# The expert stage's routing, gathers and one-hot places moved and reshaped in a two-block transformer kernel

## The chip, the cores and the metric

One core of a Trainium2 chip runs the whole program. The metric is the device time of one execution in microseconds; "before" is the median of three runs. The profile is of one execution of its own.

## What is computed

Two blocks follow each other on one sequence of 256 tokens of width 1024. The change touches only the second block, and in it the expert stage, which runs once in each of its two layers (l = 0, 1), between two layer norms:

```python
x = layer_norm(ALPHA * x + memory_cross_attention(x, mem, xq, xkv, xo), ln2_g, ln2_b)
x = layer_norm(ALPHA * x + grouped_moe(x, router_w, router_bias, e_gate, e_up, e_down), ln3_g, ln3_b)

def grouped_moe(x, ...):            # 16 experts in 4 groups
    scores = softmax(x @ router_w); biased = scores + router_bias
    # best group by the sum of its two best experts; in it, the two best experts
    ...
    for e in range(16):
        he = silu(x @ w_gate[e]) * (x @ w_up[e])
        y = y + combine[:, e:e+1] * (he @ w_down[e])
```

All arithmetic is float32. Each expert has three matrices of 1024 x 512 (2 MB each), so a layer's experts are 96 MB.

## The kernel before, in words

**Weights.** `Weights` (line 31) is a planner: all weights are 1 MB slabs in a fixed order, loaded on SyncE's DMA queue (`load`, line 66) into whatever slot came free first (`add`, `leave`). In an expert loop there are 14 slots in layer 0 and 16 in layer 1: 4 `raws`, 2 or 3 `EARLY`, 3 or 4 `MORE`, one in the place of `x`, 4 in the place of the `split` tiles. Expert slabs are used as they are (`whole`). All other weights are split before use into a high part (ScalarE, line 111) and a low part (VectorE, or GpSimd where `pool_every` says so, line 117); `next` splits `ahead` units in advance, `pace` sets `ahead`, `reach` and `settle` split at once.

**Fills.** In layer 0, key and value products of the next layer's cross attention (`key_steps`, `value_steps`) are run as fillers where TensorE would wait: `fill(n)` runs n of them. `norm2` has six in layer 0 and none in layer 1. They read `memt`, the memory's parts, which lie in the same four `turn` tiles as the gathered tokens; `memory_parts` (line 1616) makes them again after layer 0's experts.

**Routing (`moe`, line 2043).** After the second norm's statistics ScalarE scales the rows (`scale`), VectorE and GpSimd apply the norm's gain and bias to them in place (`gain`), and `both` splits them into `xth` and `xtl`, tokens on partitions. Beside that VectorE works through some twenty small operations that end in `sel` (line 2142), the chosen experts. Two matmuls (`rk`, line 2150) count the ranks; `code` is each token's place in its expert, at most 64 a pass, and a rank above 64 goes to an overflow path behind a branch (`tc.If`, line 2378) after the loop.

**The expert loop (line 2340).** Per group of four experts: `one_hot` (line 2179) makes the matrix `P2` on VectorE, `weights` (line 2200) sums each slot's share on TensorE, `turned` (line 2186) makes the transposed one-hots, `gather` (line 2216) brings the group's tokens into `XG`, in four banks evicted alternately by VectorE and ScalarE. Per expert: `into` (gate and up products, two abreast in halves of the array), `hidden` (transposes, silu, product), `down`, and `scatter` two experts later into four PSUM accumulators `y`. `scaled` adds ALPHA times the rows in three split passes. In layer 1 `last_gains` makes the last norm's gain and bias rows on TensorE. Small steps are put into the stream of weight units by a list of due times (`after`, `unit`, `rest`). The order of issue in the text of the program is the order on each engine: nothing is rescheduled. PSUM has four working banks (`bank`) in turn.

The rows' names: `P` is `P2`, `turn` is `XG`, `raw`, `w` and `x` are slots with slabs.

Of the kernel before, what the change touches and what calls it, by code (L numbers as in the profile page):

```python
# [30 lines left out]
class Weights:  # L31
# [27 lines left out]
    def fill(self):  # L59
        while self.loaded < len(self.dims):  # L60
            self.free = [f for f in self.free if f[1] is None or self.loaded < f[1]]
            if not self.free:
                return
            self.load(*self.free.pop(0))
# [340 lines left out]
def named(t, parts):  # L405

    out, o = {}, 0
    for name, n in parts:
# [11 lines left out]
        ("norm1", 1): 7}  # L420
# [12 lines left out]
def body(ctx, tc, nc, A, out):  # L433
# [896 lines left out]
    def pair(b):  # L1330
        return slice(2 * b, 2 * b + 2)
# [284 lines left out]
    def memory_parts():  # L1616

        memt = S2["memt"] = memory_tiles()
        for b in range(4):
            memt.cut(b, S2["memf"][:, pair(b), :], nc.gpsimd)  # L1620
# [422 lines left out]
    def moe(l, st, norm, steps):  # L2043
# [12 lines left out]
        ia = rt.tile([P, 2, P], F32R, name="ia")  # L2056
        nc.gpsimd.tensor_scalar(ia[:, 0, :], ident, ALPHA, None, op0=OP.mult)
        nc.vector.scalar_tensor_tensor(ia[:, 1, :], ident, ALPHA, ia[:, 0, :].bitcast(F32), op0=OP.mult, op1=OP.subtract)
# [4 lines left out]
        def small(n, name):  # L2063
            t = rt.tile([P, 2 * n], F32, name=name)
            return t.rearrange("p (t n) -> p t n", t=2)
# [11 lines left out]
        W.settle()  # L2077
        fill(1)
        XT = Parts(keep.tile([P, KD, T], F32R, name="xh"), keep.tile([P, KD, T], F32R, name="xl"))
# [7 lines left out]
        def gain(h, t, eng, part=slice(2)):  # L2087
            cs = slice(h * 512, (h + 1) * 512)
            for i, op in ((0, OP.mult), (1, OP.add))[part]:
                eng.tensor_tensor(whole[t][:, cs], whole[t][:, cs], norm.gb[:, i, cs], op=op)  # L2090

        def both(h, t, eng):
            cs = slice(h * 512, (h + 1) * 512)
            if (h, t) != (0, 0):
                nc.scalar.activation(xth[:, t, cs], whole[t][:, cs], AF.Copy)
            eng.tensor_tensor(xtl[:, t, cs], whole[t][:, cs], xth[:, t, cs].bitcast(F32), op=OP.subtract)
# [5 lines left out]
        gain(0, 0, V_, slice(1))  # L2102
        scale(0, 1)
        gain(0, 1, nc.gpsimd)
        scale(1, 1)
        scale(1, 0)
# [38 lines left out]
        gain(0, 0, V_, slice(1, 2))  # L2145
        both(0, 1, nc.gpsimd)
        nc.scalar.activation(xth[:, 0, 0:512], whole[0][:, 0:512], AF.Copy)
# [3 lines left out]
        nc.tensor.matmul(rk[:, 16:32], onesb, sel[:, 0, :], start=False, stop=True, skip_group_check=True)  # L2151
        code = small(16, "code")
# [5 lines left out]
        def count_late():  # L2158

            V_.tensor_scalar(late, code, 64.0, None, op0=OP.is_gt)  # L2160
            V_.tensor_reduce(nl, late.rearrange("p t n -> p (t n)"), op=OP.add, axis=AX.X)
            V_.tensor_tensor(late, late, comb, op=OP.mult)
            pb = bank()
            nc.tensor.matmul(pb[0:1, 0:1], nl, ones[:, 0:1], start=True, stop=True)
            V_.tensor_copy(flag, pb[0:1, 0:1])
# [43 lines left out]
        def gather(g, b, eng):  # L2209

            pb = bank()
            for j in range(2):
                c = 2 * b + j
                for i, a in enumerate((xth, xtl)):
                    for t in range(2):
                        nc.tensor.matmul(pb[:, j * T:(j + 1) * T], a[:, t, c * P:(c + 1) * P], P2s[g][:, t, :, 0:64],
                                         start=(j == 0 and i == 0 and t == 0), stop=(i == 1 and t == 1),
                                         skip_group_check=True)
            dst = XG[b][:, g % 2].rearrange("p c e s -> p (c e s)")
            if eng is nc.scalar:  # L2220
                nc.scalar.activation(dst, pb, AF.Copy)  # L2221
            else:
                eng.tensor_copy(dst, pb)


        due, count = [], [0]

        def after(n, *fs):
            due.extend((count[0] + n, f) for f in fs)

        def unit(name):
            now = [f for n, f in due if n <= count[0]]
            due[:] = [d for d in due if d[0] > count[0]]
            for f in now:
                f()
            count[0] += 1
            return W.whole(f"{name}{l}")

        def rest():
            while due:  # L2240
                due.sort(key=lambda d: d[0])
                due.pop(0)[1]()

        def into(e):

            pb = bank()
            for r in range(2):
                (wg, free_g), (wu, free_u) = unit("gate"), unit("up")
                for k in range(4):
                    if e == 0 and k % 2 == 0 and r + k:  # L2250
                        gather(0, 2 * r + k // 2, (V_, nc.scalar)[k // 2])
                    c = 4 * r + k
                    x_e = XG[c // 2][:, (e // 4) % 2, c % 2, e % 4, :]
                    for o, w in ((pb[0:64], wg), (pb[64:P], wu)):
                        nc.tensor.matmul(o, x_e, w[:, k, :], start=(c == 0), stop=(c == KD - 1), skip_group_check=True)  # L2255
                free_g()
                free_u()
            s = mo.tile([P, 512], F32, name="s", bufs=2)
            nc.scalar.activation(s, pb, AF.Copy)  # L2259
            return s  # L2260
# [27 lines left out]
        def scaled(i):  # L2288

            t, h = divmod(i, 2)  # L2290
            for k, a in ((0, xth), (0, xtl), (1, xth)):
                nc.tensor.matmul(y[i], ia[:, k, :], a[:, t, h * 512:(h + 1) * 512], start=False, stop=False,
                                 skip_group_check=True)

        def scatter(e):
            o = outs.pop(e)
            for t in range(2):
                for i in range(2):
                    for h in range(2):
                        hs = slice(64 * h, 64 * h + 64)  # L2300
                        nc.tensor.matmul(y[2 * t + h], PTs[e][hs, t * P:(t + 1) * P], o[hs, i, :],
                                         start=(e == 0 and i == 0), stop=False, skip_group_check=True)

        def last_gains(i):

            pb = bank()
            at = col[f"l{l}_ln3_{'gb'[i // 2]}_2"][0] + 4 * (i % 2)
            for c in range(4):
                nc.tensor.matmul(pb[:, c * P:(c + 1) * P], vcol[:, at + c:at + c + 1].to_broadcast([P, P]), ident,
                                 start=(c == 0), stop=(c == 3), skip_group_check=True)  # L2310
            nc.scalar.activation(norm.gb[:, i // 2, 512 * (i % 2):512 * (i % 2) + 512], pb, AF.Copy)
# [3 lines left out]
        one_hot(1, 0, 64)  # L2315
        nc.scalar.activation(codeb, code, AF.Copy)
        both(0, 0, V_)
        gain(1, 0, V_)
        gain(1, 1, nc.gpsimd)
        fill(8)  # L2320
        W.add(SlotOfSplit(), 4, W.end(f"down{l}") - 6)
        gather(0, 0, V_)
        both(1, 0, V_)
        both(1, 1, nc.gpsimd)
# [10 lines left out]

        after(1, lambda: one_hot(0, 64, 64), lambda: one_hot(1, 64, 64))
        after(2, shares)
        after(3, weights)
        after(8, count_late)
        for e in range(17):  # L2340

            g, j = divmod(e, 4)
            if e < 16:
                s = into(e)
            else:
                rest()
            if e > 1:
                scatter(e - 2)
            if e < 16 and j < 2:
                turned(j)  # L2350
            if e < 12:
                if j == 1:
                    one_hot, weights, soon = places(g + 1)
                    one_hot(0)
                    one_hot(1)
                    weights()
                if j > 1:
                    for b in (2 * j - 4, 2 * j - 3):
                        gather(g + 1, b, (V_, nc.scalar)[b % 2])
                if j == 3:  # L2360
                    turned = soon
            if e in (4, 6, 8, 10):
                scaled(e // 2 - 2)
                if last:
                    last_gains(e // 2 - 2)
            if e > 0:
                down(e - 1)
            if e < 16:
                hidden(e, s)
        rest()  # L2370
# [7 lines left out]
        with tc.If(over > 0):  # L2378
            with tc.tile_pool(name=f"ov{l}", bufs=1) as ov:

                for b in range(4):
# [8 lines left out]
                    V_.tensor_copy(x[:, pair(b), :], two(pb))  # L2390
# [42 lines left out]
    def second(xs):  # L2433
# [11 lines left out]
        with ExitStack() as st:  # L2445
            steps = chained(key_steps(), value_steps())
            y = moe(0, st, norm, steps)
# [3 lines left out]
        memory_parts()  # L2451
# [122 lines left out]
```

## Time and profile before

| | us |
|---|---|
| runs shown | 2162.61, 2173.63, 2176.61 |
| median | 2173.63 |
| profiled execution | 2169.32 |
| its span, first to last instruction | 2167.1 |

The two expert loops lie at about 1464 to 1706 and 1906 to 2151 us of the span. PE is TensorE's matmuls, PEld its weight loads, DVE VectorE, ACT ScalarE, POOL GpSimd, SP SyncE. PEclk is the granted clock as a share of 2.4 GHz. A wait names the engine and line that waits, then what ended it.

### The profile page before, as it was taken

The numbers are of one execution on the slowest core, as the hardware profiler recorded it, in microseconds if no ns is written. First come the engines' busy times: TensorE is split into PE (matmuls) and PEld (weight loads), VectorE is DVE, ScalarE is ACT, GpSimd is POOL, SyncE is SP. The second block draws the span as 40 slices with busy tenths as digits, with TensorE's granted clock in tenths as the row PEclk, the third lists the DMA queues.
The fourth block names the chain that finished last, engine by engine and source line by source line (L and its number), as shares of the span: only waits on it lengthen the run. The fifth ranks groups of instructions, "written<-read, shape, count | busy, mean of one in ns | idle before, by whom it ended". The sixth has DMA issues, their size and how long they took to land. (4 is left out here: it accounts for less than half of the span.)

```text
span 2167.1 us, 39266 instructions
## 1 busy us (share of the span) xinstructions
PE 2036.2 (94%) x16734; PEld 1696.3 (78%) x16734; DVE 1063.7 (49%) x1648; ACT 795.2 (37%) x1294; POOL 309.4 (14%) x392
## 2 busy tenths in 40 slices
PE   8999999999999999999999989998999899879996
PEld 8999888899999998888999979983434598733442
DVE  5556765655565557655655576562111276431112
ACT  5444432544454444424444544431111344211111
POOL 2112121111121112211111222110000402010000
PEclk9999999999999999999999999999999999989998
DMA  6454321254545543212544424559999445489993
GB/s 256 176 187 174 136 78 43 88 186 175 186 168 193 193 177 132 74 60 79 221 183 176 172 102 159 179 202 377 418 419 416 180 156 195 168 335 418 406 401 117
DMA packets 63209, 441.93 MB, mean 204 GB/s; under 512 B 6960, under 2 KB 7728, under 8 KB 10416
## 3 DMA queue, kind: packets, MB, share of 16 engines
q1 hardware_dynamic: 60704, 433.30, 52.3%
q10 hardware_dynamic: 1744, 3.90, 0.5%
q8 instruction: 136, 2.23, 0.4%
q0 software_dynamic: 576, 2.10, 0.3%
q14 instruction: 49, 0.40, 0.1%
HBM read 438.22 MB, written 1.05 MB: 203 GB/s over the span
## 5 line engine op out<-in xcount | busy, mean ns | idle before, releaser
L117 DVE TENSOR_TENSOR w<-raw,w 128x1024 fp32r<-128x1024 f32 (+1 forms) x426 | 520.3, 1246 | 227.5 <-ACT w L111 227.2
L530 PE MATMUL pb<-xh,w 128*128 128x256 f32 x2032 | 587.7, 289 | 3.6 <-ACT w L111 2.8
L531 PE MATMUL pb<-xl,w 128*128 128x256 f32 x2032 | 581.2, 286 | 7.9 <-DVE xl L1408 4.6
L532 PE MATMUL pb<-xh,w 128*128 128x256 f32 x2032 | 580.7, 286 | 7.6 <-DVE w L117 7.4
L111 ACT ACTIVATE w<-raw 128x1024 fp32r<-128x1024 f32 (+1 forms) x438 | 444.0, 1046 | 198.2 <-PE pb L532 108.9
L531 PEld LDWEIGHTS pb<-xl,w 128*128 128x128 f32 x2032 | 394.4, 194 | 11.6 <-DVE xl L1408 5.1
L532 PEld LDWEIGHTS pb<-xh,w 128*128 128x128 f32 x2032 | 394.2, 194 | 10.9 <-DVE w L117 10.8
L530 PEld LDWEIGHTS pb<-xh,w 128*128 128x128 f32 x2032 | 394.2, 194 | 10.1 <-ACT w L111 3.5
L532 PE MATMUL ab<-hh,w 128*128 128x256 f32 x704 | 197.9, 281 | 0.0
L530 PE MATMUL ab<-hh,w 128*128 128x256 f32 x704 | 197.9, 281 | 0.0
L531 PE MATMUL ab<-hl,w 128*128 128x256 f32 x704 | 196.3, 279 | 0.0
L2255 PE MATMUL pb<-raw,turn 128*64 128x512 f32 x712 | 178.6, 605 | 5.9 <-ACT turn L2221 2.7
L663 POOL TENSOR_TENSOR h<-sg,gu 128x256 f32<-128x256 f32 x88 | 80.8, 919 | 607.6 <-ACT sg L661 607.6
L2255 PEld LDWEIGHTS pb<-raw,turn 128*64 128x64 f32 x712 | 53.6, 138 | 106.6 <-issue 98.4
L530 PEld LDWEIGHTS ab<-hh,w 128*128 128x128 f32 x704 | 132.5, 188 | 0.2 <-issue 0.2
L531 PEld LDWEIGHTS ab<-hl,w 128*128 128x128 f32 x704 | 132.5, 188 | 0.0
L532 PEld LDWEIGHTS ab<-hh,w 128*128 128x128 f32 x704 | 132.2, 188 | 0.0
L659 DVE TENSOR_TENSOR gu<-pb,rr 128x512 f32<-128x512 f32 x88 | 60.7, 691 | 124.8 <-PE pb L532 119.8
L661 ACT ACTIVATE sg<-gu 128x256 f32<-128x256 f32 x88 | 36.7, 418 | 207.8 <-DVE gu L659 207.7
L2259 ACT ACTIVATE s<-pb 128x512 f32<-128x512 f32 x32 | 19.1, 598 | 204.5 <-PE pb L2255 204.5
L2281 PE MATMUL pb<-raw,h 128*64 128x512 f32 x368 | 94.0, 656 | 0.0
L2191 DVE TENSOR_SCALAR PT<-pb,C 128x512 fp32r<-128x512 f32 x16 | 12.0, 751 | 112.8 <-PE pb L2186 112.8
(563 smaller groups left out, 3155.4 us busy)
## 6 DMA issues: line engine op xcount, KB each, us to landing
raw<-in_wpack_dram SPq DMA_DIRECT2D x353, 1024.0 KB, 6.1
w<-in_wpack_dram SPq DMA_DIRECT2D x44, 1024.0 KB, 9.4
x<-in_wpack_dram SPq DMA_DIRECT2D x13, 1024.0 KB, 10.0
gb<-in_vecs_dram POOLq DMA_DIRECT2D x4, 512.0 KB, 5.5
C<-in_c_dram SPq DMA_DIRECT2D x1, 1041.0 KB, 16.2
xin<-in_x_dram SPq DMA_DIRECT2D x2, 512.0 KB, 5.7
mem<-in_mem_dram ACTq DMA_DIRECT2D x1, 1024.0 KB, 9.3
out_dram<-xout SPq DMA_DIRECT2D x4, 256.0 KB, 2.1
```

Source lines behind the costliest of these rows:

```text
L111: self.nc.scalar.activation(h, src, AF.Copy)
L117: (self.nc.gpsimd if pool else self.nc.vector).tensor_tensor(lo, src, h.bitcast(F32), op=OP.subtract)
L530: nc.tensor.matmul(o, wh, xh, start=first, stop=False, skip_group_check=True)
L531: nc.tensor.matmul(o, wh, xl, start=False, stop=False, skip_group_check=True)
L532: nc.tensor.matmul(o, wl, xh, start=False, stop=last, skip_group_check=True)
L659: nc.vector.tensor_tensor(gu, two(pb), rr[:, None, :].to_broadcast([P, 2, T]), op=OP.mult)
L661: nc.scalar.activation(sg, gu[:, 0, :], AF.Silu)
L663: nc.gpsimd.tensor_tensor(h, sg, gu[:, 1, :], op=OP.mult)
L2191: V_.tensor_scalar(PT, two(pb), c2["slotp"], None, op0=OP.is_equal)
L2255: nc.tensor.matmul(o, x_e, w[:, k, :], start=(c == 0), stop=(c == KD - 1), skip_group_check=True)
L2259: nc.scalar.activation(s, pb, AF.Copy)
L2281: nc.tensor.matmul(pb[64 * n:64 * n + 64], h[:, 2 * r + k, :], w[:, k, n * 512:(n + 1) * 512], start=(r == 0 and k == 0), stop=(r == 1 and ...
```

## The change

Gain and bias of norm 2 no longer go into the rows before the split: `xth` and `xtl` are parts of the plain normalized rows, and gain and bias (now per partition) are applied where `gather` evicts a bank, half by VectorE, half by ScalarE. The rows with gain, which `scaled` needs, are made later by eight VectorE steps in expert 0; `scaled` is then one full float32 product per bank, all four in expert 1. GpSimd has no work in the routing. In layer 1 thirty warm-up matmuls stand ahead of `rk`. Two gathers instead of one stand ahead of the loop. In a group, one-hots are made in its first expert, weights in its second, and the gathers are spread 0, 1, 2, 1 over the four. `scatter` follows `down` instead of preceding it. The count of late tokens moves behind expert 2. `memory_parts` is called in expert 15 of layer 0 with VectorE instead of GpSimd, and two fill units are split ahead of the branch. `last_gains` becomes a broadcast load from HBM on GpSimd's queue, at expert 13. The list of due times is gone. In the overflow path the evictions apply gain and bias too.

```diff
-        ("norm1", 1): 7}
+        ("norm1", 1): 7, ("route", 1): 30}
-            memt.cut(b, S2["memf"][:, pair(b), :], nc.gpsimd)
+            memt.cut(b, S2["memf"][:, pair(b), :], nc.vector)
...
-        ia = rt.tile([P, 2, P], F32R, name="ia")
...
+        ia = rt.tile([P, P], F32, name="ia")
+        nc.gpsimd.tensor_scalar(ia, ident, ALPHA, None, op0=OP.mult)
...
         W.settle()
+        W.pace(0)
         fill(1)
...
+        def first_part(h, t):
+            cs = slice(h * 512, (h + 1) * 512)
+            nc.scalar.activation(xth[:, t, cs], whole[t][:, cs], AF.Copy)
+        def second_part(h, t):
+            cs = slice(h * 512, (h + 1) * 512)
+            V_.tensor_tensor(xtl[:, t, cs], whole[t][:, cs], xth[:, t, cs].bitcast(F32), op=OP.subtract)
...
-        gain(0, 0, V_, slice(1))
         scale(0, 1)
-        gain(0, 1, nc.gpsimd)
-        scale(1, 1)
-        scale(1, 0)
+        first_part(0, 0)
+        first_part(0, 1)
+        for t in range(2):
+            scale(1, t)
+        for t in range(2):
+            first_part(1, t)
...
         fill(2)
-        gain(0, 0, V_, slice(1, 2))
-        both(0, 1, nc.gpsimd)
-        nc.scalar.activation(xth[:, 0, 0:512], whole[0][:, 0:512], AF.Copy)
+        warm("route", l)
...
+        second_part(0, 0)
         code = small(16, "code")
...
-            dst = XG[b][:, g % 2].rearrange("p c e s -> p (c e s)")
...
+            for j in range(2):
+                dst = XG[b][:, g % 2, j].rearrange("p e s -> p (e s)")
+                gv, bv = vec(norm.g, 0, 2 * b + j), vec(norm.b, 0, 2 * b + j)
+                if j:
+                    nc.scalar.activation(dst, pb[:, T:], AF.Identity, scale=gv, bias=bv)
+                else:
+                    V_.tensor_scalar(dst, pb[:, :T], gv, bv, op0=OP.mult, op1=OP.add)
...
-                    if e == 0 and k % 2 == 0 and r + k:
-                        gather(0, 2 * r + k // 2, (V_, nc.scalar)[k // 2])
+                    if e == 0 and c in (2, 4):
+                        gather(0, c // 2 + 1)
...
-            for k, a in ((0, xth), (0, xtl), (1, xth)):
-                nc.tensor.matmul(y[i], ia[:, k, :], a[:, t, h * 512:(h + 1) * 512], start=False, stop=False,
+            nc.tensor.matmul(y[i], ia, whole[t][:, h * 512:(h + 1) * 512], start=True, stop=False, skip_group_check=True)
...
+                nc.gpsimd.dma_start(norm.gb[:, i, :], rows[at:at + D].partition_broadcast(P))
...
+        second_part(0, 1)
         nc.scalar.activation(codeb, code, AF.Copy)
-        both(0, 0, V_)
-        gain(1, 0, V_)
-        gain(1, 1, nc.gpsimd)
+        W.pace(2)
         fill(8)
...
-        gather(0, 0, V_)
-        both(1, 0, V_)
-        both(1, 1, nc.gpsimd)
+        gather(0, 0)
+        second_part(1, 0)
+        gather(0, 1)
+        second_part(1, 1)
...
         for e in range(17):
...
+            if e == 0:
+                one_hot(0, 64, 64)
+                one_hot(1, 64, 64)
+                shares()
+                weights()
+                late_shares()
+                for i in range(4):
+                    gain(i % 2, i // 2)
+            if e == 1:
+                for i in range(4):
+                    scaled(i)
+            if e == 15 and ending is not None:
+                ending()
+            if e == 16:
+                scatter(14)
+            if e > 0:
+                down(e - 1)
+            if e == 16:
+                W.pace(2)
+                W.reach(2)
+                W.settle()
+            elif e > 1:
                 scatter(e - 2)
             if e < 16 and j < 2:
                 turned(j)
+            if e == 2:
+                count_late()
             if e < 12:
-                if j == 1:
+                if j == 0:
                     one_hot, weights, soon = places(g + 1)
                     one_hot(0)
                     one_hot(1)
+                elif j == 1:
                     weights()
-                if j > 1:
-                    for b in (2 * j - 4, 2 * j - 3):
-                        gather(g + 1, b, (V_, nc.scalar)[b % 2])
+                for b in ([], [0], [1, 2], [3])[j]:
+                    gather(g + 1, b)
...
-            if e in (4, 6, 8, 10):
-                scaled(e // 2 - 2)
-                if last:
-                    last_gains(e // 2 - 2)
-            if e > 0:
-                down(e - 1)
+            if last and e == 13:
+                last_gains()
             if e < 16:
                 hidden(e, s)
```

## Rows read from the trace of the kernel before

**Rows 1.** the page, parts 1 and 5: engines, and splitting a weight

```profile
PE 2036.2 (94%) x16734; PEld 1696.3 (78%) x16734; DVE 1063.7 (49%) x1648; ACT 795.2 (37%) x1294; POOL 309.4 (14%) x392
...
L117 DVE TENSOR_TENSOR w<-raw,w 128x1024 fp32r<-128x1024 f32 (+1 forms) x426 | 520.3, 1246 | 227.5 <-ACT w L111 227.2
...
L111 ACT ACTIVATE w<-raw 128x1024 fp32r<-128x1024 f32 (+1 forms) x438 | 444.0, 1046 | 198.2 <-PE pb L532 108.9
```

**Rows 2.** stretches: us; busy PE, PEld, DVE, ACT, POOL; PEclk, DMA, GB/s

```profile
1520.00:1540.00 20.00, 20.00 (x109) 8.73 (x107) 2.52 (x4) 2.76 (x5) 0.00 (x0) 1.00 1.00 413
...
1540.00:1560.00 20.00, 18.20 (x88) 7.43 (x88) 4.27 (x8) 2.52 (x5) 0.00 (x0) 0.91 1.01 423
...
1464.40:1480.30 15.90, 13.73 (x66) 6.53 (x67) 4.33 (x12) 1.19 (x2) 1.04 (x1) 0.89 0.89 371
...
1890.00:1900.00 10.00, 0.20 (x2) 0.10 (x1) 8.95 (x29) 3.91 (x7) 6.03 (x6) 0.66 1.02 427
...
1905.90:1922.30 16.40, 14.19 (x66) 6.59 (x67) 4.41 (x12) 1.27 (x3) 1.57 (x1) 0.86 0.57 220
```

**Rows 3.** waits of PE, layer 0, 1430:1720: us, times, longest

```profile
PE pb L2200 <- DVE P L2179: 5.4, 6, 1.5
...
PE pb L2150 <- DVE sel L2142: 3.6, 1, 3.6
...
PE pb L2255 <- ACT turn L2221: 1.4, 2, 0.7
...
PE pb L2255 <- ACT xh L2095: 0.8, 1, 0.8
...
PE pb L2255 <- DVE turn L2223: 0.8, 1, 0.8
...
PE pb L2164 <- DVE nl L2161: 0.7, 1, 0.7
```

**Rows 4.** waits of PE, layer 1, 1880:2167

```profile
PE pb L2150 <- DVE sel L2142: 11.3, 1, 11.3
...
PE pb L2255 <- DVE turn L2223: 1.6, 2, 0.8
```

**Rows 5.** timeline at experts 5 and 15, layer 0: start, us, engine

```profile
1550.08 1.28 DVE L2179 TENSOR_TENSOR P<-C,code 128x512 fp32r<-128x512 f32 x2
...
1550.91 0.24 PE L2200 MATMUL pb<-comb,P 128*128 128x2 f32 x1 [1.54 <-DVE P L2179]
...
1552.55 5.04 PE L2281 MATMUL pb<-raw,h 128*64 128x512 f32 x16
...
1693.57 3.65 PE L2281 MATMUL pb<-raw,h 128*64 128x512 f32 x16
```

**Rows 6.** timeline of both layers' routing

```profile
1445.82 0.18 DVE L2124 TENSOR_TENSOR two_max<-bi 128x16 f32<-128x16 f32 x1
...
1893.87 1.22 DVE L2124 TENSOR_TENSOR two_max<-bi 128x16 f32<-128x16 f32 x1
...
1895.14 1.28 POOL L2090 TENSOR_TENSOR ol<-ol,gb 128x512 f32<-128x512 f32 x1
...
1899.94 1.12 DVE L2138 TENSOR_SCALAR top<-ahead 128x32 f32<-128x32 f32 x1
```

**Rows 7.** timeline: expert 4 of layer 1, and warm-ups after the middle norm

```profile
1977.52 0.48 PE L2292 MATMUL ab<-xh,ia 128*128 128x512 f32 x1
...
1978.30 1.06 PE L2309 MATMUL pb<-ident,vcol 128*128 128x128 f32 x8
...
1727.98 1.24 PE L523 MATMUL pb<-identb 128*128 128x512 bf16 x5 [1.03 <-ACT x L1452]
```

**Rows 8.** groups by line from 1300 on: a gain step on DVE

```profile
L2090 DVE TENSOR_TENSOR oh<-oh,gb 128x512 f32<-128x512 f32 x8 | 5.5, 687 | 1.8 <-ACT oh L2085 1.8
```

**Rows 9.** stretches: the middles of both loops, columns as in rows 2

```profile
1528.00:1682.00 154.00, 150.39 (x760) 60.54 (x758) 21.55 (x38) 18.58 (x35) 0.00 (x0) 0.98 1.00 413
...
1943.00:2117.00 174.00, 170.39 (x884) 72.79 (x882) 23.24 (x40) 23.73 (x44) 0.00 (x0) 0.98 0.99 403
```

More of the change, by code (lines that the diff above doesn't have):

```diff
@@ L2041, in tile, with moe @@
             return split.tile([P, 2, 1024], F32, name="w").rearrange("p c t -> p (c t)")
-    def moe(l, st, norm, steps):
+    def moe(l, st, norm, steps, ending=None):
         nonlocal x
@@ L2054, in moe @@
         fill = filler(steps, l, "norm2")
-        ia = rt.tile([P, 2, P], F32R, name="ia")
-        nc.gpsimd.tensor_scalar(ia[:, 0, :], ident, ALPHA, None, op0=OP.mult)
-        nc.vector.scalar_tensor_tensor(ia[:, 1, :], ident, ALPHA, ia[:, 0, :].bitcast(F32), op0=OP.mult, op1=OP.subtract)
+        ia = rt.tile([P, P], F32, name="ia")
+        nc.gpsimd.tensor_scalar(ia, ident, ALPHA, None, op0=OP.mult)
         trib, onesb = rt.tile([P, P], BF16, name="trib"), rt.tile([P, P], BF16, name="onesb")
@@ L2085, in scale, with gain @@
             nc.scalar.activation(whole[t][:, cs], norm.zt[2 * t + h], AF.Identity, scale=r[:, t:t + 1], bias=nm[:, t:t + 1])
-        def gain(h, t, eng, part=slice(2)):
+        def first_part(h, t):
             cs = slice(h * 512, (h + 1) * 512)
-            for i, op in ((0, OP.mult), (1, OP.add))[part]:
-                eng.tensor_tensor(whole[t][:, cs], whole[t][:, cs], norm.gb[:, i, cs], op=op)
-        def both(h, t, eng):
+            nc.scalar.activation(xth[:, t, cs], whole[t][:, cs], AF.Copy)
+        def second_part(h, t):
             cs = slice(h * 512, (h + 1) * 512)
-            if (h, t) != (0, 0):
-                nc.scalar.activation(xth[:, t, cs], whole[t][:, cs], AF.Copy)
-            eng.tensor_tensor(xtl[:, t, cs], whole[t][:, cs], xth[:, t, cs].bitcast(F32), op=OP.subtract)
+            V_.tensor_tensor(xtl[:, t, cs], whole[t][:, cs], xth[:, t, cs].bitcast(F32), op=OP.subtract)
+        def gain(h, t):
+            cs = slice(h * 512, (h + 1) * 512)
+            for i, op in ((0, OP.mult), (1, OP.add)):
+                V_.tensor_tensor(whole[t][:, cs], whole[t][:, cs], norm.gb[:, i, cs], op=op)
         V_.tensor_reduce(mx, sc, op=OP.max, axis=AX.X, negate=True)
@@ L2156, in moe, with late_shares @@
         flag = rt.tile([1, 1], I32, name="flag")
-        def count_late():
+        def late_shares():
             V_.tensor_scalar(late, code, 64.0, None, op0=OP.is_gt)
@@ L2162, in count_late @@
             V_.tensor_tensor(late, late, comb, op=OP.mult)
+        def count_late():
             pb = bank()
@@ L2207, in moe, with gather @@
         XG = [S2["turns"].tile([P, 2, 2, 4, 64], F32, name=f"turn{b}") for b in range(4)]
-        def gather(g, b, eng):
+        def gather(g, b):
             pb = bank()
@@ L2218, in gather @@
                                          skip_group_check=True)
-            dst = XG[b][:, g % 2].rearrange("p c e s -> p (c e s)")
[L2220 to L2229, printed above, removed]
-        def unit(name):
[L2232 to L2236, printed above, removed]
+            for j in range(2):
[5 more added lines that the diff above has]
+                    V_.tensor_scalar(dst, pb[:, :T], gv, bv, op0=OP.mult, op1=OP.add)
+        def unit(name):
             return W.whole(f"{name}{l}")
[L2239 to L2242, printed above, removed]
         def into(e):
@@ L2290, in scaled @@
             t, h = divmod(i, 2)
-            for k, a in ((0, xth), (0, xtl), (1, xth)):
-                nc.tensor.matmul(y[i], ia[:, k, :], a[:, t, h * 512:(h + 1) * 512], start=False, stop=False,
-                                 skip_group_check=True)
+            nc.tensor.matmul(y[i], ia, whole[t][:, h * 512:(h + 1) * 512], start=True, stop=False, skip_group_check=True)
         def scatter(e):
@@ L2301, in scatter, with last_gains @@
                         nc.tensor.matmul(y[2 * t + h], PTs[e][hs, t * P:(t + 1) * P], o[hs, i, :],
[L2302 to L2311, printed above, removed]
+                                         start=False, stop=False, skip_group_check=True)
+        def last_gains():
+            rows = A["vecs"].rearrange("r p -> (r p)")
+            for i, k in enumerate("gb"):
+                at = col[f"l{l}_ln3_{k}_2"][0] * P
+                nc.gpsimd.dma_start(norm.gb[:, i, :], rows[at:at + D].partition_broadcast(P))
         one_hot, weights, turned = places(0)
@@ L2334, in shares @@
             V_.tensor_tensor(comb2[:, :, :, 1], comb, comb2[:, :, :, 0].bitcast(F32), op=OP.subtract)
[L2336 to L2339, printed above, removed]
         for e in range(17):
@@ L2344, in moe @@
                 s = into(e)
-            else:
-                rest()
-            if e > 1:
+            if e == 0:
[20 more added lines that the diff above has]
+            elif e > 1:
                 scatter(e - 2)
@@ L2355, in moe @@
                     one_hot(1)
+                elif j == 1:
                     weights()
-                if j > 1:
-                    for b in (2 * j - 4, 2 * j - 3):
-                        gather(g + 1, b, (V_, nc.scalar)[b % 2])
+                for b in ([], [0], [1, 2], [3])[j]:
+                    gather(g + 1, b)
                 if j == 3:
                     turned = soon
-            if e in (4, 6, 8, 10):
-                scaled(e // 2 - 2)
-                if last:
-                    last_gains(e // 2 - 2)
-            if e > 0:
-                down(e - 1)
+            if last and e == 13:
+                last_gains()
             if e < 16:
                 hidden(e, s)
-        rest()
         scatter(15)
@@ L2389, in moe @@
                                                  skip_group_check=True)
-                    V_.tensor_copy(x[:, pair(b), :], two(pb))
+                    for c in (2 * b, 2 * b + 1):
+                        nc.scalar.activation(x[:, c, :], pb[:, (c % 2) * T:(c % 2 + 1) * T], AF.Identity,
+                                             scale=vec(norm.g, 0, c), bias=vec(norm.b, 0, c))
                 for e in range(16):
@@ L2446, in second @@
             steps = chained(key_steps(), value_steps())
-            y = moe(0, st, norm, steps)
+            y = moe(0, st, norm, steps, memory_parts)
         right.close()
@@ L2450, in second @@
         S2["V"] = kv.tile([P, 2, D], F32, name="V")
-        memory_parts()
         xs = mid_norm(y, filler(steps, 1, "norm3"))
```

## Prediction

> **What bounds the kernel now.** The page's busy line comes first: PE is busy in 94% of the span, DVE in half of it, POOL in 14% [rows 1]. PE is the bound over the whole, and time can come only from stretches where PE waits, runs at a low clock, or does work that goes away. So the second view is the stretches of the two expert loops [rows 2]. In the middle of layer 0's loop PE is either full at a granted clock of 1.00 (1520 to 1540) or short by 1.8 us at a mean clock of 0.91 (1540 to 1560). In layer 1 there is a hole: from 1890 to 1900 PE works 0.2 us, and its clock falls. The DMA share is 0.9 to 1.0 in all four loop or routing stretches but one: the weights run close to their own limit, and that is the thing to fear for any gain on PE. The third view, PE's waits, names the causes [rows 3, 4]: the weight products `L2200` wait six times per layer for the one-hot `P` on DVE, 5.4 us; the rank product `L2150` waits for `sel`, 3.6 us in layer 0 and 11.3 us in layer 1; expert 0 waits four times for a gathered `turn` or what it is made of, 3.0 us in each layer (0.8 + 0.8 + 1.4, and 1.6 + 1.4); the overflow count waits 0.7 us for `nl`. No wait for a weight slab is among them.
>
> **Part by part.** The sum is made against the profiled execution, 2169.3 us (span 2167.1 and 2.2 around it); the median of the runs shown, 2173.6, is 4.3 above it.
>
> *One-hot places in other steps.* Before, in the second expert of each group of four, DVE writes the next group's one-hots (1.28 us for two), PE waits 1.54 us plus a short second wait, and makes the weight products [rows 5]. Now the one-hots are issued in the group's first expert, and the products one expert later, a whole `into` of PE work behind them. The waits go: 5.4 us per layer, 10.8 in all. Each was also followed by a stretch at half clock (1.2 of 2.4 GHz): the `down` after it takes 5.04 us where an undisturbed one takes 3.65 [rows 5]. One fall costs at least that difference, 1.4 us, and at most the 0.09 of 20 us that the stretch shows, 1.8 [rows 2]; I take 1.7. Three per layer: 10.2 us. The count moves behind expert 2's other work: its wait goes too, 0.7 per layer, 1.4.
>
> *Expert 0's gathers.* Two gathers now run before the first expert, so the second covers the first one's eviction, and each later gather stands two row blocks ahead of its reader. Each eviction is halved between DVE and ACT. The four waits go, 3.0 us per layer, 6.0. Expert 0 also ran at a mean clock of 0.89 in layer 0 and 0.86 in layer 1 [rows 2]: 0.11 of 15.9 us and 0.14 of 16.4 us, 1.7 and 2.3; with no waits and, in layer 1, warm-ups ahead, I count all of it, 4.0. The scale and bias ride on evictions that exist anyway. The DVE work that expert 0 gains, eight gain steps of 0.69 us [rows 8], 5.5 us, lies beside expert 1's `into`. Its reader `scaled` stands behind that `into`. If the cover failed, PE would wait up to those 5.5 us once per layer.
>
> *Routing without POOL.* DVE's small operations are stretched while POOL adds: `two_max` takes 0.18 us in layer 0 and 1.22 in layer 1, in the midst of POOL's gain additions, of which one is shown; it is the first of five stretched ones in layer 1, and `top`, 1.12, the last [rows 6]. Five times 1.04 is 5.2 us off the chain that ends at `sel`. In layer 1 PE has nothing to do in that time, so all of it counts. Thirty warm-up matmuls fill the hole: five took 1.24 us [rows 7], so thirty take 7.4 at full clock, against a hole of 11.3 - 5.2 = 6.1. They would end 1.3 us late, which I set against the clock that they keep up in the one-hots and gathers before expert 0; there the second gather fits in the time that one took at half clock, 1.0 us gained.
>
> In layer 0 the same stretch is covered by fill products up to the 3.6 us wait. That wait goes, but the pace of 0 leaves the next three fill units unsplit until `sel` is done: the first then needs 1.05 us on ACT and 1.25 on DVE in series [rows 1] behind ACT's four scales and four first parts. I see a new stall of almost the same length. Bounds: -1.5 us (it is longer, and the clock falls all the same) to +4.2 (no stall); I take 0.8, near the nearest rows, which are those two splits.
>
> *Residual.* Before, a `scaled` is three passes, started 0.78 us ahead of what follows it [rows 7], 3.1 us per layer. Now it is four full-precision products. The trace has no such form at this size, but `down` is sixteen instructions of 512 columns, two abreast, in 3.65 us [rows 5]: eight in a row, which is what four products of full width need. So +0.5 per layer, -1.0 in all (bounds 0 and -1.4).
>
> *Last gains.* Four times eight transposing products of about 1.0 us [rows 7] leave PE in layer 1: 4.0 us. The broadcast load that takes their place is 1 MB on POOL's queue at expert 13, and its reader comes after the loop: nothing.
>
> *Memory's parts.* They move from behind layer 0's overflow test to expert 15, on ACT and DVE, beside `down`; four DVE steps like those of rows 8 are 2.8 us against 3.65 of cover. Two fill units are split there too. PE was waiting for the branch at that place, not for them: nothing.
>
> Sum: 10.8 + 10.2 + 1.4 + 6.0 + 4.0 + 5.2 + 1.0 + 0.8 - 1.0 + 4.0 = 42.4. 2169.3 - 42.4 = 2126.9, rounded to 2127.
>
> **The rivals.**
>
> *The weights become the bound.* In the middles of the loops the DMA share is 1.00 and 0.99 at 413 and 403 GB/s [rows 9], 2.54 and 2.60 us a slab, 15.2 and 15.6 us for an expert's six. If that is a ceiling, what is saved in the middle is spent waiting for slabs: two waits and falls per layer, 4 x (1.8 + 1.7) = 14, and the 4.0 of the last gains. For it: share 1.00. Against it: no PE wait names a slab, 14 and 16 slots hold them, so a reserve is there to be eaten, and rows 2 show 423 GB/s. Price 18 us: 2145.
>
> *The routing hole stays.* If the clock is low when the warm-ups start, thirty of them take twice 7.4 us, end 8.7 us after `sel` is done (14.8 - 6.1), and the rank product waits in PE's queue behind them; with layer 1's 2.3 us of clock in expert 0 that is 11 us: 2138. For it: the clock in that stretch is 0.66 [rows 2]. Against it: it falls only after the hole has begun, and the warm-ups have no operand to wait for.
>
> *The change does not do what it says in the groups.* The one-hots now stand in DVE's queue ahead of the multiply for `h`. If `down` then waits for the 1.28 us of the two one-hots [rows 5] and the clock falls as before, six moves cost 6 x (1.28 + 1.7) = 18 us: 2145. Against it: the next `into`, twice as long as the one-hots, lies between.
>
> *Slower: the clock flutters.* Every fall costs 1.7 us, and 42.4 / 1.7 = 25 falls in the 32 experts cancel the gain; with 1.5 falls per expert, 48, the time is 2127 + 82 = 2209. The place is the loop: the new order hands each bank from `down` to `scatter`, `turned` and gathers with less other work between. For it: one wait of 1.54 us was enough for a fall [rows 5]. Against it: 1520 to 1540 holds 1.00 with the same four banks in turn [rows 2]. The Trainium skill, in "TensorE: Matmul & The Clock Gate", section "A second HAM failure mode: psum-queue depth-cycling", speaks for this rival: a kernel that cycles PSUM banks lets TensorE idle briefly so often that its clock swings between its two levels. Here the trace disagrees, by the 1.00 just named; by that rule the time would be the 2209.
>
> **How the numbers follow.** Forecast 0.62, weights 0.16, routing 0.11, groups 0.07, flutter 0.04. The forecast alone spans 2115 to 2141. Downward: 3.4 us if layer 0 has no stall, and 6.7 by which the shortest run shown lies under the profiled one. Upward: 2.3 if layer 0's stall is at its other bound, 2.0 if six falls were worth 1.4 each, 1.3 of warm-ups, and 7.3 of the longest run. The range goes down to 2112 and up to 2149, the 2145 of two rivals with the 4.3 of the median. A change of 1%, some 21.7 us, is about what a measurement of this kernel tells from none; it would be at 2151.9. The forecast and the next three cases are all below that, 0.96, less 0.05 for two of them at once: faster 0.91; same 0.06, slower 0.03, the flutter parted by its number of falls.
>
> **What would show it.** Right: no `L2200` wait for `P`, clock 1.00 from expert 1 to the end of each loop, PE's wait for `sel` near zero in both layers, loops shorter by about 15 and 20 us (the terms above by layer). Wrong: PE waits that name a weight slab (first rival), a gap between the warm-ups' end and `sel` or the reverse (second), waits for `h` (third), a clock below 1.00 in any loop stretch without a wait (fourth). If the time is above 2149, the step that failed is the loop's middle.

## The result, and the profile after

The kernel after takes 2117.6 us (median of four runs, 2113.1 to 2118.9), the kernel before 2173.2 beside it: a ratio of 0.975, interval 0.971 to 0.979. A second series gave 2111.2 against 2166.3, 0.974 (0.971 to 0.977). The forecast was 2127, and its own range, 2115 to 2141, holds the time; it is 9 us too long.

The profiled execution after took 2116.8 (span 2115.0). By stage, in us, read from the trace (the start of the last transposing product of the norm ahead of it, `L1368`, opens a routing; the first gate product ends it; the last scatter ends a loop):

| stage | before | after | gain | forecast |
|---|---|---|---|---|
| layer 0 routing | 26.2 | 22.8 | 3.4 | 0.8 |
| layer 0 loop | 241.5 | 222.2 | 19.3 | 15.4 |
| layer 1 routing | 16.8 | 11.0 | 5.8 | 6.2 |
| layer 1 loop | 245.3 | 220.9 | 24.4 | 20.0 |
| all else | 1637.3 | 1638.1 | -0.8 | 0 |
| span | 2167.1 | 2115.0 | 52.1 | 42.4 |

"All else" hides two opposite differences. Ahead of the first routing, which the change doesn't touch, the profile after is 4.2 us longer, with 44.4 us at half clock there against 27.3. Between layer 0's loop and layer 1's routing it is 3.3 us shorter; 0.9 of that is a wait for VectorE behind the branch (`L531` for `xl`) that is gone, the rest was not assigned.

The stretches that answer to [rows 2, 9], same columns, and the engine line of the page:

```profile
PE 2016.1 (95%) x16724; PEld 1692.6 (80%) x16724; DVE 1067.3 (50%) x1680; ACT 803.0 (38%) x1306; POOL 284.9 (13%) x376
...
1520.00:1540.00 20.00, 20.00 (x104) 7.59 (x104) 3.91 (x7) 2.51 (x5) 0.00 (x0) 1.00 1.02 422
...
1465.20:1474.90 9.70, 9.70 (x50) 4.10 (x49) 4.38 (x14) 2.05 (x4) 0.00 (x0) 1.00 0.99 393
1868.30:1874.90 6.60, 6.60 (x34) 3.03 (x33) 4.94 (x31) 4.87 (x10) 0.73 (x1) 1.00 1.01 427
1878.40:1888.10 9.70, 9.70 (x50) 4.12 (x49) 4.36 (x14) 2.04 (x4) 0.00 (x0) 1.00 1.02 421
1500.00:1660.00 160.00, 160.00 (x854) 67.23 (x852) 26.52 (x48) 25.37 (x47) 0.00 (x0) 1.00 1.01 420
1920.00:2080.00 160.00, 160.00 (x848) 66.43 (x848) 26.52 (x48) 25.76 (x48) 0.00 (x0) 1.00 1.01 420
```

PE is never idle in the 160 us in the middle of either loop, and its clock stays at 1.00, in expert 0 (1465 and 1878) too. In exchange the DMA share, 1.00 and 0.99 in [rows 9] at 413 and 403 GB/s, is 1.01 at 420 GB/s. PE's waits, layer 0 from the rank product to the branch, and layer 1, against [rows 3, 4]:

```profile
PE pb L530 <- PEq L2378: 5.8, 1, 5.8
PE pb L2247 <- DMA x<-in_wpack_dram: 1.6, 1, 1.6
PE pb L530 <- ACT w L111: 1.5, 1, 1.5
...
PE ab L2291 <- ACT ol L2277: 0.8, 1, 0.8
PE pb L532 <- DVE w L117: 0.8, 1, 0.8
```
```profile
PE pb L2222 <- DVE P L2185: 0.8, 1, 0.8
...
PE pb L2247 <- DMA x<-in_wpack_dram: 0.2, 1, 0.2
```

Every wait of [rows 3, 4] is gone. New are 0.8 us for the first one-hots ahead of layer 1's gathers, the split of a fill unit behind layer 0's rank product (1.5 + 0.8) and a wait for a weight slab. This last wait stands in expert 15, and the row shows only its first stop; the whole of it is read from the products (timeline of PE, layer 0):

```profile
1660.08 3.60 PE L2273 MATMUL pb<-raw,h 128*64 128x512 f32 x16
1663.61 1.19 PE L2291 MATMUL ab<-oh,PT 64*128 64x512 f32 x8
1664.74 0.66 PE L2259 MATMUL pb<-ident,s 128*128 128x128 f32 x4
1665.33 4.50 PE L2247 MATMUL pb<-raw,turn 128*64 128x512 f32 x18
1671.40 0.64 PE L2247 MATMUL pb<-x,turn 128*64 128x512 f32 x1 [1.57 <-DMA x<-in_wpack_dram]
...
1678.41 1.20 PE L2291 MATMUL ab<-ol,PT 64*128 64x512 f32 x8
```

From the start of an `into` to the scatter behind its `down` a plain expert takes 10.45 us; here it is 13.08 (1665.33 to 1678.41): 2.6 us lost to slabs in layer 0, and by the same reading 1.3 in layer 1. The reserve of landed slabs, 12.7 us at its smallest before in layer 0 (from each slab's landing to its first product), is eaten to nothing.

### The profile page after: what moved, and what is told of

The parts are those of the page before. It is cut to its first block, busy times and chain, and to the rows that moved or that the text cites. A ratio compares the mean times of both kernels' runs of the same rounds, so it can differ in the third digit from the quotient of the medians.

```text
span 2115.0 us, 39279 instructions
## 1 busy us (share of the span) xinstructions
PE 2016.1 (95%) x16724; PEld 1692.6 (80%) x16724; DVE 1067.3 (50%) x1680; ACT 803.0 (38%) x1306; POOL 284.9 (13%) x376
## 5 line engine op out<-in xcount | busy, mean ns | idle before, releaser
L531 PE MATMUL pb<-xl,w 128*128 128x256 f32 x2032 | 582.0, 286 | 7.0 <-DVE xl L1408 4.6
L532 PEld LDWEIGHTS pb<-xh,w 128*128 128x128 f32 x2032 | 395.2, 194 | 11.4 <-DVE w L117 11.3
L531 PEld LDWEIGHTS pb<-xl,w 128*128 128x128 f32 x2032 | 395.5, 195 | 10.7 <-DVE xl L1408 5.1
L530 PEld LDWEIGHTS pb<-xh,w 128*128 128x128 f32 x2032 | 395.4, 195 | 10.2 <-ACT w L111 3.8
L531 PE MATMUL ab<-hl,w 128*128 128x256 f32 x704 | 196.3, 279 | 0.0
L531 PEld LDWEIGHTS ab<-hl,w 128*128 128x128 f32 x704 | 132.6, 188 | 0.0
L2278 DVE SCALAR_TENSOR_TENSOR ol<-pb,ws,ol 128x512 fp32r<-128x512 f32 x16 | 12.0, 751 | 147.7 <-ACT ol L2277 147.7
L2273 PE MATMUL pb<-raw,h 128*64 128x512 f32 x368 | 85.1, 593 | 0.0
```

The source lines that it names most:

```text
L530: nc.tensor.matmul(o, wh, xh, start=first, stop=False, skip_group_check=True)
L531: nc.tensor.matmul(o, wh, xl, start=False, stop=False, skip_group_check=True)
L532: nc.tensor.matmul(o, wl, xh, start=False, stop=last, skip_group_check=True)
L2273: nc.tensor.matmul(pb[64 * n:64 * n + 64], h[:, 2 * r + k, :], w[:, k, n * 512:(n + 1) * 512], start=(r == 0 and k == 0), stop=(r == 1 and ...
L2278: V_.scalar_tensor_tensor(o[:, 1], pb, wss[e], o[:, 0].bitcast(F32), op0=OP.mult, op1=OP.subtract)
```

## The experiments

Totals of one kernel, as changed, scatter by up to 9 us. Much of that lies outside the stages of the change: ahead of the first routing the profiles after have 24 to 44 us at half clock, and that stretch takes 1435.6 us in the one with least and 1442.4 in the one with most. So stages are compared. Where nothing in layer 0's routing or loop was edited (five profiles), its loop took 222.1 to 223.4 us. In two profiles of the kernel after, layer 1's loop took 220.9 and 220.3 us, and from the transposing to its end 231.9 and 231.3. Differences below are taken against the first of these profiles. The runs pe_load, slots_minus, pool_busy, no_warm, gains_late and pace1 are one execution each.

**The stop for the one-hots.**

```diff
-                if j == 0:
+                if j == 1:
                     one_hot, weights, soon = places(g + 1)
                     one_hot(0)
                     one_hot(1)
-                elif j == 1:
                     weights()
```


> The kernel after, with the next group's one-hots and the weight products both in the group's second expert, after `turned`, as in the kernel before. In the two traces the stretch from the start of `turned` to the end of the weight products took 3.57 us before and 1.10 after, and the `down` behind it 4.96 against 3.53. Theory A (the stop costs its whole 2.5 us of PE and brings a fall of the clock, 1.4 us, three times in each layer; the 2.6 and 1.3 us that PE now waits for weight slabs at expert 15 are given back): 6 x 3.9 - 3.9 = 19.5, so about 2137 us, three falls inside each loop, loops of about 231 and 231 us. Theory B (the falls came from the old order of `scatter` and `down`, not from this wait): the falls stay away, 6 x 2.5 - 3.9 = 11, about 2128.5. Theory C (only the 5.4 us per layer of the wait rows counted, the clock is a matter of chance): 10.8 - 3.9 = 7, about 2124.5.

Measured: 2135.9 us (2132.0 to 2138.4; 0.984 of before, 0.981 to 0.987); loops 232.1 and 231.9, +9.9 and +11.0.

```diff
                     one_hot(1)
+                    warm("places", l)
                     weights()
```


> As onehot_back, with ten warm-up matmuls (0.22 us each, 2.2 in all) between `turned` and the weight products, so that PE works through the wait for the one-hots. The work of the experts and the place of the one-hots are those of onehot_back; only what PE does in the wait differs. Theory A (a wait costs its own time, and a second, separate price for the clock that falls in it): no falls in the loops, each stop costs about the same 2.4 us as without warm-ups, so the time lies some 8 us under onehot_back (6 x 1.4), about 2128. Theory B or C (the clock doesn't hang on this wait): the same time as onehot_back, within 2 us.

Measured: 2123.7 us (0.978 of before, 0.975 to 0.981); loops 227.4 and 227.1. The timeline of layer 0, first of onehot_back (the first line is of the group before), then with the warm-ups at the same place:

```profile
1490.06 0.24 PE L2206 MATMUL pb<-comb,P 128*128 128x2 f32 x1 [2.59 <-DVE P L2185]
...
1545.77 0.40 PE L2192 MATMUL pb<-identb,codeb 128*128 128x128 bf16 x4
1547.98 0.24 PE L2206 MATMUL pb<-comb,P 128*128 128x2 f32 x1 [1.81 <-DVE P L2185]
1548.49 0.94 PE L2206 MATMUL pb<-comb,P 128*128 128x2 f32 x7 [0.27 <-DVE P L2185]
```
```profile
1545.59 0.40 PE L2192 MATMUL pb<-identb,codeb 128*128 128x128 bf16 x4
1545.82 2.32 PE L523 MATMUL pb<-identb 128*128 128x512 bf16 x10
1547.79 0.35 PE L2206 MATMUL pb<-comb,P 128*128 128x2 f32 x1
1548.30 0.94 PE L2206 MATMUL pb<-comb,P 128*128 128x2 f32 x7 [0.16 <-DVE P L2185]
```

The one-hots come no earlier, but PE works in place of waiting. The clock then fell in neither loop. In onehot_back it fell after all three stops of layer 0's loop (10.2 us at half clock), but in layer 1's after the first two alone (6.8 and 3.4 us), where theory A had three. Otherwise theory A holds, with both prices apart: the falls 4.7 + 4.8 = 9.5 us, and the stops 5.2 + 6.2 = 11.4, to which the 3.9 us come that PE no longer waits for slabs (no wait of the two runs' loops names one): 15.3, or 2.5 per stop. Three of the six stops are longer here than in the kernel before: 2.59, 2.59 and 1.81 us of first wait in place of 1.53, since DVE there first evicts the result of the `down` just before (0.75 us, at 1487.90 and 1545.83 in layer 0).

**Who bounds the loops.** In what follows the edge is the point from which the stream of weight slabs, and no longer PE, sets when a loop ends.

```diff
+            if e == 8:
+                warm("extra", l)
```


> The kernel after with nine more warm-up matmuls (about 2.0 us of PE work) in expert 8 of each layer. Theory of the edge (the weights' stream now ends last: PE only waits less at expert 15): layer 0's loop stays at 222.2 us with expert 15's wait for a slab gone or under 0.5 us; layer 1's loop grows by 0.7 (it has 1.3 us of such waiting to give), 221.6. Rival (PE is still what bounds the loops, and expert 15's wait is a chance of one slab): both loops grow by 2.0, to 224.2 and 222.9, and the wait of 1.6 us stays in layer 0.

Measured: loops 221.8 and 221.6. Two us more of PE work cost layer 0 nothing, and no PE wait names a slab any more; layer 1 paid 0.7. That is what the theory of the edge said.

```diff
-MORE = (3, 4)
+MORE = (2, 3)
```


> The kernel after with one slot fewer for weight slabs in each layer (2 and 3 instead of 3 and 4 of the extra ones). Theory of the edge, by the stream: in layer 0 the stream stands still for some 2.5 us ahead of the loop because no slot is free, and one slot fewer makes that one slab longer, so every later slab comes 2.5 us later, and the loop ends 2.5 us later, 224.7 us; in layer 1 the stream never stands still, so a slot fewer changes nothing, 220.9. Rival 1 (the reserve is the number of slots): both loops grow by 2.5. Rival 2 (the slabs don't bound the loops): both stay within 0.3 us.

Measured: loops 225.3 and 221.6, +3.1 and +0.7. PE's waits in layer 0's loop:

```profile
PE pb L2247 <- DMA raw<-in_wpack_dram: 2.6, 2, 1.3
```

Layer 0 went as the stream's theory says (a low stretch in its routing also brought its first expert 2.8 us later; in pool_busy, where that was 1.5, the loop stayed at 222.3), layer 1 nearly (0.7 for 0, about as much as its two profiles above differ; what remains is open). In these two layers it counted when the stream stands still, and not only how many slots there are. The Trainium skill, "DMA: Bandwidth & Descriptors", section "Where 436 GB/s comes from", puts the fabric's ceiling at 435 GB/s and names a lower limit of about 358 for one core's HBM reads. The trace agrees with the first alone: 420 GB/s over 160 us.

```diff
-                nc.gpsimd.dma_start(norm.gb[:, i, :], ...
+                nc.sync.dma_start(norm.gb[:, i, :], ...
...
-            if last and e == 13:
+            if last and e == 15:
```


> The kernel after with the last norm's gain and bias rows loaded on SP's queue at expert 15 of layer 1, behind the last weight slab, and not on POOL's queue, where they were issued at 1894.7 us, in the second expert. In the kernel after, slabs 19 to 21 of layer 1 land 3.1, 3.8 and 3.1 us apart in place of 2.5. Theory (the stream of slabs bounds the loop's end, and 1 MB beside it delays every later slab by 2.5 us): the last slab lands 212.2 us after the loop's start (214.7 with the load in the midst), expert 15 doesn't wait for a slab, layer 1's loop takes 219.6 us in place of 220.9. Rival (the load took a spare share of the queues): the last slab lands 214.7 us after the loop's start as before and the loop stays at 220.9.

Measured: the last slab 211.8 us after the loop's start, loop 219.6, no slab wait. The row of the kernel after that shows the load's place (timeline of POOL):

```profile
1894.70 1.26 POOL L2299 DMA_DIRECT2D gb<-in_vecs_dram  x2 [25.10 <-DVE ol L2099]
```

Written at expert 13, it ran in the second expert: POOL has nothing else to do, and waits for the last gain step alone. The stretch behind the loop was 0.7 us longer here (16.4 against 15.7). DVE's last step ends 12.4 us after the loop in both, so the difference lies behind it, where the result is stored; why is open.

**Routing.**

```diff
+            for i in range(8):
+                nc.gpsimd.tensor_tensor(idle, norm.gb[:, 0, 0:256], norm.gb[:, 1, 0:256], op=OP.add)
         V_.tensor_tensor(two_max, b4[:, :, 0:2], b4[:, :, 2:4], op=OP.max)
```


> The kernel after with eight additions of 128x256 on POOL, into a tile that nobody reads, beside layer 1's routing chain on DVE. POOL's additions of 128x512 took 1.28 us before, so these take about 0.65 each, 5.2 in all. Theory (DVE's small operations stand still while POOL adds, whatever it adds): the chain from the mean to `sel`, 4.9 us in the kernel after, becomes about 9 to 10 us, single operations are stretched to some 0.6 us each, and since the thirty warm-ups end after 6.6 us, PE waits about 4 us for `sel`; layer 1's stretch from the middle of the chain to the rank product grows by that. Rival (the chain was long because its data or its operands came late, by the norm's gain steps and ACT): POOL's work changes nothing, the chain stays within 0.5 us of 4.9 and PE's wait for `sel` stays away.

Measured: `sel` comes 3.0 us later and the loop ends 3.5 us later. Timeline:

```profile
1866.08 4.76 POOL L2132 TENSOR_TENSOR idle<-gb 128x256 f32<-128x256 f32 x6
...
1868.62 0.62 DVE L2133 TENSOR_TENSOR two_max<-bi 128x16 f32<-128x16 f32 x1
...
1869.17 0.16 DVE L2134 TENSOR_TENSOR two_sum<-bi 128x16 f32<-128x16 f32 x1
```

Six operations were stretched, by about 0.5 us each (`two_max` 0.62, in the kernel after 0.17); their neighbours, like `two_sum`, passed at 0.16 while POOL was at work. The cause is POOL. The size is about two thirds of what was expected: as we read the rows, an operation that meets an addition waits for it, but several pass between two. The Trainium skill, "SBUF — State Buffer", section "Terms", calls this an exclusive lock held for a whole instruction. The stretched rows agree; the chain as a whole doesn't lose POOL's whole busy time (3.0 of 6.4 us).

```diff
-        ("norm1", 1): 7, ("route", 1): 30}
+        ("norm1", 1): 7}
```


> The kernel after without the thirty warm-up matmuls ahead of layer 1's rank product. Theory (the warm-ups hold the clock, the chain on DVE sets the time): PE waits about 5.5 us for `sel`, the rank product itself starts 0.2 us earlier, the clock falls ahead of the loop as in the kernel before, the gathers and expert 0 run partly at half clock: rank product to first expert 4.4 us where it was 3.6, expert 0 2 us longer, of which the 1.3 us of waiting for slabs at expert 15 are given back; in all about 1.5 us, at most 3. Rival (the clock stays up, as it did over the waits of 1.5 us at expert 15 and in layer 0's routing): the loop stays at 220.9 and the time is the same.

Measured: PE waits 6.2 us for `sel`; first expert 1.2 us later; expert 0 at 1.00; loop 219.7; loop's end 231.9 us after the transposing, with and without warm-ups. Stretches: hole, gathers, expert 0.

```profile
1861.00:1868.40 7.40, 1.22 (x12) 1.14 (x11) 5.50 (x33) 4.67 (x9) 0.73 (x1) 0.63 0.94 380
1868.40:1873.30 4.90, 3.93 (x18) 3.71 (x18) 3.06 (x7) 1.39 (x4) 0.00 (x0) 0.52 1.03 428
1873.40:1883.00 9.60, 9.60 (x50) 4.04 (x49) 4.11 (x13) 1.69 (x3) 0.00 (x0) 1.00 1.01 418
```

Without warm-ups the clock is low for the one-hots and gathers, as the theory says, but not in expert 0, and PE gets the 1.2 us back at expert 15: the stream sets the end.

```diff
-        W.pace(0)
+        W.pace(1)
```


> The kernel after with one unit split ahead in the routing, where it is none. In layer 0 the stall behind the rank product, 1.5 us for ACT's part and 0.8 for DVE's, then goes. Theory (the split fits beside the chain; the stream of slabs bounds layer 0's loop): rank product to first expert 11 us in place of 13.3, and the loop grows by what the stream doesn't start earlier, 0 to 2.3 us, so that the time is 0 to 2.3 us shorter. Rival (the split takes ACT and DVE from the chain, as in the kernel before): the rank product waits again for `sel`, 2 us or more, the clock falls, and the stretch up to the first expert is as long as it was.

Measured: first expert as in the kernel after (22.8), stall 1.1 + 0.8, loop 221.4. Neither theory came true: the unit in question is still split behind ACT's scales.

**A version from these.**

> The kernel after once more, beside the next run on the same chip. Every theory expects 2117.6 us within some 3 us. Counted from the transposing of the rows ahead of each routing (the same instruction in both layers), its profiles had the loops' ends at 245.0 and 231.9 us; theory: these two come again within 0.3 and 0.1 us for layer 1 and within 1 for layer 0, and what scatters in the total is the number of clock falls elsewhere.

```diff
+        if not last:
+            W.reach(3)
         for t in range(2):
             scale(1, t)
...
+            if e == 15:
+                scatter(13)
             if e < 16:
                 s = into(e)
...
-            elif e > 1:
+            elif 1 < e < 15:
                 scatter(e - 2)
```
(and the two lines of gains_late)

> The kernel after with three edits that work on the two streams' ends. In layer 0's routing the next fill unit is split on ACT ahead of the second pair of scales, which takes away the stall behind the rank product (2.3 us) and lets the stream of slabs go on 2.3 us earlier; in expert 15 the scatter of expert 13 stands ahead of the gate and up products, so that 1.1 us of it lie in the wait for slabs; the last gains are loaded behind the last slab, as in gains_late. Theory of the edge: layer 0's loop ends 2 to 3.4 us earlier, counted from the transposing ahead of the routing (245.0, so 241.6 to 243), layer 1's 1.3 us earlier (231.9, so 230.6); the total is 3 to 5 us under after_again, about 2113. Rival (the slabs of layer 0 come no earlier, since the stream goes on only when a later unit is done): layer 0's end moves by the scatter's 1.1 us alone, 243.9, and the total by 2.4.

Measured, same chip: after_again 2111.2 us (2109.6 to 2119.0), this one 2110.6 (2109.4 to 2115.0; 0.974 of before, 0.970 to 0.977). The stage in layer 0 moved as expected: end of loop at 241.9 us after the transposing, in after_again 246.3 (in the kernel after 245.0). Layer 1's didn't (231.4 for 231.3): after_again lost 0.7 us to slabs in its expert 15, not 1.3, and the scatter moved ahead waits 0.5 us for its eviction. The medians can't be told apart: it beats before, not measurably after. The forecast for after_again itself was missed: 6.4 us less in total, and ends of loops 1.3 and 0.5 us off, more than was allowed.

## Why the prediction was right or wrong

*One-hot places in other steps.* Right in mechanism; the term of the stops was mis-sized. The waits of [rows 3] gave 10.8 us. In the timeline of the kernel before, the six stretches from the start of `turned` to the product behind the weight products take 4.04, 3.57 (1548.98 to 1552.55, in [rows 5]), 3.31, 4.04, 3.31 and 3.32 us; after, each takes 1.10 (one is 1544.70 to 1545.80). That is 15.0 us, or 13.5 without the count's two waits of 0.7, which lie in the 4.04: 2.2 to 2.5 a stop. The 15.3 of onehot_back_warm are those of its own, partly longer stops. A wait row starts at the end of the last product and so leaves out the overlap of neighbours that a stop also costs: after, the four transposes take 0.40 us, but the first weight product starts 0.21 after their start. The falls, priced at 10.2, measured 9.5 in onehot_back, with as long at half clock (20.5 us in both loops) as those behind the six stops before.

*Expert 0's gathers.* From the first expert's start to the second's: 17.2 and 17.6 us before, 11.3 after in both. Of these 6 us, 1.0 is the gather that now stands ahead of the loop, which the sum had no term for; the rest agrees with the 3.0 of waits and the 1.7 and 2.3 of clock, as priced. No run parts these; they are read from the two traces. The cover for the gain steps held.

*Routing.* `sel` comes 5.1 us earlier in layer 1 (12.2 against 7.1 after the transposing), the 5.2 of the sum. Thirty warm-ups took 6.6 us, not 7.4. Their price and use were set against each other; both are small, and no_warm shows that the use is nothing while the stream sets the end. In layer 0 the choice of 0.8 was too low: the new stall is 2.3 us, not almost the old 3.6, and the clock mostly stayed up over it; the 3.4 gained lies in the bounds given.

*Residual, last gains.* The four products take 3.6 us a layer (3.3 and 2.9 before): -1.0 as priced; the 3.9 of the transposing products went. "Its reader comes after the loop: nothing" failed in two ways: the load ran in the second expert, and it costs the weights' stream 2.5 us, of which 0.7 to 1.3 show (219.6 in gains_late against 220.3 and 220.9). Memory's parts were costed at nothing: the branch held PE for 5.9 us before and 5.8 after. Whether the 3.3 us gained behind it come from them is not shown.

*The rivals.* The weights do become the bound, but later and cheaper than that rival had it: one wait per layer at the end of the reserve, 3.9 us and not 14, with no fall of the clock. There is no bank flutter: 1.00 over 160 us twice. No PE wait names `h`, and the warm-ups ran at 1.00 and let the rank product start 0.3 us behind `sel`, so the other two rivals didn't come either.

So the loops' 8.3 us beyond the forecast are 2.7 of stops, 2.2 of expert 0 (2.0 of it the moved gathers), 3.2 of transposes and scatters (1.0 and 0.6 us less a layer, summed from the start of each product to the next), 2.6 of gate and up products (by the same sum 7.02 us an expert before and 6.92 after, in experts 2 to 14) and 1.5 not assigned, less the 3.9 of slabs. Why transposes, scatters, gate and up products run closer is not shown.

*The range.* The bounds that the prediction lists add up to 2117 and 2140, not 2115 and 2141, and its 2112 has no sum. The measured 2117.6 lies at the edge of what its terms allow; that the range holds it owes something to luck, since gains that had no term and the wait for slabs, which stood only among the rivals, partly cancel.

## What to carry to other kernels

Price a stop of TensorE by the stretch around it in a run where it is absent, not by the wait row: here 2.2 to 2.5 us for rows of 1.8, and 1.6 more for the clock. Before summing gains of one engine, lay the transfer stream beside it: count when it last stands still and when its last slab must land, since from that edge on a saved microsecond is only a longer wait. A DMA issue runs where its engine gets to it, not where it stands in the text.

## What the runs showed of the hardware

The clock doesn't follow from the length of a wait alone. The stop for the one-hots, 1.5 us of waiting among products of two columns, was followed by half clock six times of six before and five times of six in onehot_back; the one without a fall has the same two waits, 1.53 and 0.27 us, as two of the others there. The wait for a slab behind full products late in the loop, 1.3 to 1.6 us, was followed by no fall in six profiles. The stall in layer 0's routing, there in ten of the profiles after (1.5 + 0.8 us, in pace1 1.1 + 0.8), brought a low stretch in three of them and cost 1.5 to 2.8 us more (first expert at 24.4 to 25.6 in place of 22.8). The branch behind the loop holds PE for 5.2 to 6.9 us in layer 0 in the twelve profiles, though the overflow is empty.
